# A decoder layer on one core: the first channels as two single chunks, three blocks held in PSUM, weights packed in 4 KB runs

## The chip, the cores and the metric

The kernel runs on one core of a Trainium2 chip. A core has five engines with queues of their own: TensorE (PE; PEld is its weight load), VectorE (DVE), ScalarE (ACT), GpSimd (POOL) and SyncE (SP), and 16 DMA engines that bring data from HBM into SBUF. TensorE writes its sums into PSUM, eight banks of 128 partitions x 512 floats. The metric is the device time of one execution in microseconds (us); a profiled execution gives the trace. In the profile, L156 is line 156 of the kernel before, "whi" and "wlo" are the two halves of a weight, "acc" and "misc" are PSUM banks.

## What is computed

One layer of a hybrid decoder, 256 tokens by 2048 channels, all in float32:

```python
mod = silu(c) @ w_ada + b_ada                      # (1, 12288)
shift1, scale1, gate1, shift2, scale2, gate2 = split(mod, 6)
h = rms_norm(x, norm1_gain) * (1 + scale1) + shift1
proj = h @ w_in                                    # 2048 -> 13840 columns
# stick-breaking attention, dilated attention and gated linear attention on columns of proj,
# each projected to 2048, gated by sigmoid(gate columns of proj), summed
x = x + gate1 * (mixed @ w_out)
h = rms_norm(x, norm2_gain) * (1 + scale2) + shift2
gate, up = split(h @ w_ffn_in, 2)
x = x + gate2 * ((silu(gate) * up) @ w_ffn_out)
```

## The kernel before

**Matmuls.** Each float32 factor is split in two: `hi`, rounded to TensorE's fast float32 format, and `lo`, the rest. A product is three matmuls, hi x hi, hi x lo and lo x hi (`mm3`, lines 153 to 156). A *block* is 512 output columns; its two token tiles of 128 accumulate in two PSUM banks. A *chunk* is 128 input channels. One chunk of one block is thus six matmuls of 128 x 512. `load_weights` (lines 125 to 151) loads two chunks (512 KB) with one DMA on SP's queue into one of four `raw` buffers; ScalarE casts them to `whi` (L148), DVE subtracts to get `wlo` (L149). There are four buffers of each.

**The input projection.** The normalised input needs shift1 and scale1, for which 16 tiles of w_ada for every channel chunk must be read and multiplied by silu(c). So that the projection can start early, its 16 channel chunks go in groups, `GROUPS` = (0,3), (3,7), (7,11), (11,16). One pass over 13 blocks uses one group; meanwhile `ada_group` (lines 277 to 310) reads w_ada for the next one (L291) and DVE multiplies and adds (L269, L271), spread over the pass; then TensorE turns the sums (L321), DVE reduces them (L322) and finishes shift and scale (L328, L331), and `make_h` (lines 424 to 436) writes hi (L429) and lo (L436) of h, both tiles of a chunk at once. A block's result of the first pass is copied by ScalarE from PSUM to SBUF (`A[b]`, L473); the next passes add theirs to it on DVE (L475). In the last pass ScalarE copies `A[b]` into the PSUM banks before the block (L461, "seeded"), and the matmuls add to that. The last block of a pass stays in PSUM and is the first of the next ("carried").

**The start.** `first_group` (lines 487 to 553) issues on SP's queue: three tiles of w_ada for chunks 0 to 2 (384 KB each), the first weight tile, x (four DMAs of 512 KB, L375), the other 13 tiles of w_ada. `norm1` (lines 380 to 411) sums the squares of x on ScalarE (L387), makes 1/rms, puts it on a scaled identity (L404), and TensorE multiplies x by it, which transposes and scales x (L410); ScalarE copies the result to `xT` (L411). DVE adds the 16 products, columns of chunk 0 last by themselves; ones sum them over the partitions (L313), and h of chunk 0 follows; chunks 1 and 2 go by way of transposes (L538) and sums (L541). Between these, `keep_warm` (lines 413 to 417) lets TensorE multiply ones, 78 matmuls in all, whose result nobody reads.

**PSUM.** Four banks are "acc" (the blocks), four "misc" (everything else).

**The order of the work.** Each engine runs its own instructions in a fixed order, which a scheduler made from priorities (`prio`) and the edges that `issue_after` adds. The weights, x and w_ada all go through SP's queue in this order; the small vectors through SP's and GpSimd's.

**Later.** The last pass has the two attentions and the gated linear attention between its blocks; the r blocks (columns 13 and 14, `gla`'s output gate) and the 12 gate blocks follow with all 16 chunks at once; then the branch projections, `w_out`, and the feed-forward part.

Of the kernel before, what the change touches and what calls it, by code (L numbers as in the profile page):

```python
# [17 lines left out]
P = 128  # L18
# [15 lines left out]
DEFER = 4  # L34
AHEAD = 4000
WARM = (22, 43, 10, 3)
FIN = 13
GROUPS = ((0, 3), (3, 7), (7, 11), (11, 16))
# [3 lines left out]
ROW_N1, ROW_N2, ROW_SBQ, ROW_SBK, ROW_DILQ, ROW_DILK, ROW_GB, ROW_GG = 16, 32, 48, 49, 50, 51, 52, 56  # L42
# [24 lines left out]
def trunk(ctx: ExitStack, tc: tile.TileContext, I, out):  # L67
# [57 lines left out]
    def load_weights(src, k0, k1, c0, w=NB, spare=(), ahead=True):  # L125
# [32 lines left out]
    def block(pss, act, src, k0, k1, c0, base=0, w=None, tiles=range(NT), go_on=False, more=False, seeded=False):  # L158

        if w is None:  # L160
            w = load_weights(src, k0, k1, c0)
# [27 lines left out]
    nc.scalar.preload_act_table_set("natural_log_exp_and_others")  # L189
# [7 lines left out]
    nc.sync.dma_start(crow[0:KC, :], by_chunk("c"))  # L197
# [12 lines left out]
    vec = const.tile([P, 58], F32, name="vec")  # L210
    bada = const.tile([P, 96], F32, name="bada")

    def load_vectors():
        nc.sync.dma_start(rows[16:32, :], by_chunk("norm1_gain"))
        nc.sync.dma_start(brow[0:96, :], by_chunk("b_ada"))
        nc.sync.dma_start(rows[32:48, :], by_chunk("norm2_gain"))
        with tc.issue_after(made):
# [9 lines left out]
            nc.gpsimd.dma_start(rows[0:16, :], by_chunk("c"))  # L227

    def turn_vectors():
        cols_ps = misc_bank([P, 64])  # L230
        nc.tensor.transpose(cols_ps[:, :58], rows[:58, :], ident[:58, :58])
        nc.scalar.copy(vec, cols_ps[:, :58])
        bada_ps = misc_bank([P, 96])
        state["row_turn"] = nc.tensor.transpose(bada_ps, brow[:96, :], ident[:96, :96])
        nc.scalar.copy(bada, bada_ps)
# [28 lines left out]
    w_ada = I["w_ada"]  # L264
# [12 lines left out]
    def ada_group(k0, k1, tags=ADA_TAGS, between=None):  # L277
# [5 lines left out]
        for i in range(pieces):  # L283
# [4 lines left out]
            for k in range(KC):  # L288
                with prio():
                    raw = S(tags[count % len(tags)], [P, 2, w])  # L290
                    nc.sync.dma_start(  # L291
                        raw,
                        w_ada[k * P : (k + 1) * P, : 2 * D].rearrange("p (s c) -> p s c", s=2)[:, :, a * P : a * P + w],
                    )
# [53 lines left out]
    def ada_segment_steps(acc, seg, done):  # L348


        for k in range(KC):
            for j in range(2):
# [3 lines left out]
                c0 = seg * D + j * 2 * NB  # L356
# [23 lines left out]
    def norm1():  # L380
# [21 lines left out]
        for t in range(NT):  # L402
            act(col(r, t), col(y, t), AF.Copy, scale=col(z, t))
            act(diag[:, t, :], ident, AF.Copy, scale=col(r, t))  # L404
        for j in range(4):
            for t in range(NT):
                ps = misc_bank([P, 4, P])
                for i in range(4):
                    xs = xin[2 * t + j // 2][:, j % 2, i * P : (i + 1) * P]
                    state["turn"] = nc.tensor.matmul(ps[:, i, :], xs, diag[:, t, :], start=True, stop=True)  # L410
                state["turned"] = nc.scalar.copy(xT[j][:, :, t * P : (t + 1) * P], ps)  # L411

    def keep_warm(n):

        ps = acc_bank()
        for _ in range(n):
            state["warm"] = nc.tensor.matmul(ps, ones_r, wide, start=True, stop=True)
# [26 lines left out]
    A = [None] * 13  # L444

    up, down = list(range(13)), list(range(12, -1, -1))
    orders = (up[1:] + up[:1], up, down)
# [4 lines left out]
    def proj_block(g, b, w=None, carry=False):  # L452
        k0, k1 = GROUPS[g]
        go_on = bool(carried)
        pss = carried.pop() if go_on else [acc_bank() for _ in range(NT)]
        seeded = g == LAST and not go_on
        if seeded:

            with prio():
                for t in range(NT):  # L460
                    nc.scalar.copy(pss[t], A[b][:, t, :])  # L461
            go_on = True
        block(pss, h_at, w_in, k0, k1, b * NB, w=w, go_on=go_on, more=carry, seeded=seeded)
        if carry:
            carried.append(pss)
            return
        with prio():
# [3 lines left out]
            for t in range(NT):  # L471
                if first or seeded:
                    nc.scalar.copy(A[b][:, t, :], pss[t])  # L473
                else:
                    nc.vector.tensor_add(A[b][:, t, :], A[b][:, t, :], pss[t])  # L475

# [10 lines left out]
    def first_group():  # L487


        k0, n = GROUPS[0]  # L490
        w = n * P
        tags = tuple(f"A{j}" for j in range(9)) + ADA_TAGS
        raws = []

        def load(ks):
            for k in ks:
                raw = S(tags[k % len(tags)], [P, 2, w])
                nc.sync.dma_start(raw, w_ada[k * P : (k + 1) * P, : 2 * D].rearrange("p (s c) -> p s c", s=2)[:, :, :w])
                raws.append(raw)

        load(range(0, 3))
        early.extend(load_weights(w_in, 0, 2, orders[0][0] * NB, ahead=False))
        split = state["split"]
        load_x()
        load(range(3, KC))
        with tc.issue_after(c_turn.ins):
            keep_warm(WARM[0])
        with tc.issue_after(state["warm"].ins):
            turn_vectors()
        with tc.issue_after(state["row_turn"].ins):  # L510
            keep_warm(WARM[1])
        norm1()
        with tc.issue_after(state["turn"].ins):
            keep_warm(WARM[2])
        acc = S("ada", [P, 2, w])
        for k in range(KC - 1):
            with tc.issue_after(split.ins) if k > 3 else nullcontext():
                ada_mac(acc, raws[k], k)
        sh, sc = mod1[:, 0, 0:n], mod1[:, 1, 0:n]
        chunk = lambda q: slice(q * P, (q + 1) * P)  # L520

        def last_mac(q):
            return ada_mac(acc[:, :, chunk(q)], raws[KC - 1][:, :, chunk(q)], KC - 1)

        last_mac(0)
        last_mac(1)
        behind = state["warm"]
        for q in range(n):
            if q == 0:
                sums = misc_bank([P, 2])  # L530
                for j in range(2):
                    with tc.issue_after(behind.ins):
                        behind = column_sum(sums[:, j : j + 1], acc[:, j, chunk(q)])
            else:
                ps = misc_bank([P, 2, P])
                for j in range(2):
                    with tc.issue_after(behind.ins):
                        behind = nc.tensor.transpose(ps[:, j, :], acc[:, j, chunk(q)], ident)  # L538
                sums = small([P, 2])
                with tc.issue_after(state["h_lo"].ins):  # L540
                    nc.vector.reduce_sum(sums, ps, axis=AX.X)  # L541
            finish_columns(sums[:, 0:1], sh[:, q : q + 1], SEG_SHIFT1, q)
# [748 lines left out]
```

## Time and profile before

| | |
|---|---|
| median of 3 runs | 1621.04 us (1619.27 to 1621.42) |
| the profiled execution, from first to last instruction | 1619.6 us |
| TensorE clock granted, mean | 0.998 |
| HBM read | 392.53 MB |
| moved by the DMA engines | 395.94 MB, mean 244 GB/s |
| DMA issues of w_in | 205 of 512 KB, 26 of 256 KB |

The page's busy shares are means over stages with different limits. A matmul's recorded length includes its way through the array, and matmuls overlap: the spacing of their starts, not the length, says how fast they go.

### The profile page before, as it was taken

To read this page: it belongs to the slowest core of one execution; us is meant where nothing else is said; L and a number is where in the kernel's file an instruction comes from. 1 tells how busy PE (TensorE), PEld (TensorE's weight loads), DVE (VectorE), ACT (ScalarE), POOL (GpSimd) and SP (SyncE) were. 2 spreads that over 40 slices of the span, in tenths; PEclk is the share of its full clock that TensorE was granted. 3 is DMA by queue.
4 is the path that set the end of the run, shared out by engine and by line. 5 is a ranking of instruction groups with operands and counts; after the bars stand their busy time and mean duration, and the time that the engine had idled before them with its cause. 6 is when DMAs were issued, how large, how long until landed. Compare 5 with 4: busy or idle time off the path is not lost.

```text
span 1619.6 us, 19955 instructions
## 1 busy us (share of the span) xinstructions
PE 1602.4 (99%) x7353; PEld 1324.3 (82%) x7353; DVE 1123.5 (69%) x1301; ACT 798.8 (49%) x1110; POOL 5.3 (0%) x14
## 2 busy tenths in 40 slices
PE   8999999999999999999999999999999999999998
PEld 7878888788888888888887888888888888888887
DVE  6899995887888787878657566677655555454454
ACT  4654449755795434444445444444444444333332
POOL 1000000000000000000000000000000000000000
PEclk9999999999999999999999999999999999999999
DMA  9999997884876889898756577888666666666663
GB/s 321 339 336 321 330 313 241 283 263 131 272 235 221 302 304 311 304 305 302 237 191 202 152 240 254 276 269 263 207 190 187 189 188 187 190 206 193 206 207 111
DMA packets 194593, 395.94 MB, mean 244 GB/s; under 512 B 12914, under 2 KB 27928, under 8 KB 194496
## 3 DMA queue, kind: packets, MB, share of 16 engines
q1 hardware_dynamic: 194272, 394.67, 74.8%
q8 instruction: 57, 0.93, 0.2%
q14 instruction: 40, 0.33, 0.1%
q0 software_dynamic: 224, 0.01, 0.0%
HBM read 392.53 MB, written 2.10 MB: 244 GB/s over the span
## 4 chain that ended last, share of the span: by engine, by line
PE 87%; DVE 5%; DMA 3%; ACT 3%; issue 2%; SPq 0%; DVEq 0%; ACTq 0%
PE acc L156 27%; PE acc L154 27%; PE acc L155 27%; DVE wlo L149 2%; ACT whi L148 1%; DVE ada L271 1%; DMA AR<-w_ada 1%; PE misc L1061 1%; ACT scr L616 1%; PE misc L775 1%; DMA OS<-w_ada 1%; DMA A<-w_ada 1%; DVE T L271 0%; DMA raw<-w_br_gla 0%; DMA raw<-w_in 0%
## 5 line engine op out<-in xcount | busy, mean ns | idle before, releaser
L149 DVE TENSOR_TENSOR wlo<-raw,whi 128x1024 fp32r<-128x1024 f32 (+1 forms) x546 | 651.6, 1198 | 421.4 <-ACT whi L148 420.2
L148 ACT CAST whi<-raw 128x1024 fp32r<-128x1024 f32 (+1 forms) x546 | 562.5, 1032 | 703.5 <-PE acc L156 583.1
L154 PE MATMUL acc<-whi,H 128*128 128x512 f32 x1576 | 616.6, 392 | 0.4 <-ACT H L1143 0.4
L156 PE MATMUL acc<-whi,H 128*128 128x512 f32 x1576 | 616.0, 391 | 1.0 <-DVE H L1144 0.6
L155 PE MATMUL acc<-wlo,H 128*128 128x512 f32 x1576 | 615.7, 391 | 1.0 <-DVE wlo L149 1.0
L156 PEld LDWEIGHTS acc<-whi,H 128*128 128x128 f32 x1576 | 296.1, 188 | 63.1 <-DVE H L436 1.5
L155 PEld LDWEIGHTS acc<-wlo,H 128*128 128x128 f32 x1576 | 296.4, 188 | 61.8 <-DVE wlo L149 1.8
L154 PEld LDWEIGHTS acc<-whi,H 128*128 128x128 f32 x1576 | 296.4, 188 | 60.3 <-ACT H L1143 0.6
L154 PE MATMUL acc<-whi,A 128*128 128x512 f32 x312 | 121.9, 391 | 0.0
L155 PE MATMUL acc<-wlo,A 128*128 128x512 f32 x312 | 121.5, 389 | 0.3 <-DVE wlo L149 0.3
L156 PE MATMUL acc<-whi,A 128*128 128x512 f32 x280 | 109.0, 389 | 0.0
L271 DVE SCALAR_TENSOR_TENSOR ada<-AR,csil,ada 128x1024 f32<-128x1024 f32 x59 | 75.1, 1278 | 5.8 <-DMA AR<-w_ada 5.8
L155 PEld LDWEIGHTS acc<-wlo,A 128*128 128x128 f32 x312 | 58.6, 188 | 12.7 <-DVE wlo L149 0.7
L154 PEld LDWEIGHTS acc<-whi,A 128*128 128x128 f32 x312 | 58.6, 188 | 11.9
L156 PEld LDWEIGHTS acc<-whi,A 128*128 128x128 f32 x280 | 52.6, 188 | 11.0
L154 PE MATMUL acc<-whi,T 128*128 128x512 f32 x120 | 46.7, 389 | 0.0
L155 PE MATMUL acc<-wlo,T 128*128 128x512 f32 x120 | 46.7, 389 | 0.0
L156 PE MATMUL acc<-whi,T 128*128 128x512 f32 x120 | 46.7, 389 | 0.0
L156 PE MATMUL acc<-whi,OS 128*128 128x512 f32 x112 | 43.6, 389 | 0.0
L271 DVE SCALAR_TENSOR_TENSOR ada<-OS,csil,ada 128x1024 f32<-128x1024 f32 (+2 forms) x33 | 35.5, 1077 | 1.8 <-DMA OS<-w_ada 1.5
L473 ACT COPY A<-acc 128x512 f32<-128x512 f32 x50 | 29.0, 586 | 10.2 <-PE acc L156 9.1
L475 DVE TENSOR_TENSOR A<-A,acc 128x512 f32<-128x512 f32 x48 | 31.5, 682 | 2.0 <-PE acc L156 1.8
(347 smaller groups left out, 1228.8 us busy)
## 6 DMA issues: line engine op xcount, KB each, us to landing
raw<-w_in SPq DMA_DIRECT2D x205, 512.0 KB, 5.3
raw<-w_ffn_in SPq DMA_DIRECT2D x176, 512.0 KB, 4.0
raw<-w_ffn_out SPq DMA_DIRECT2D x88, 512.0 KB, 4.7
AR<-w_ada SPq DMA_DIRECT2D x79, 512.0 KB, 5.3
raw<-w_out SPq DMA_DIRECT2D x32, 512.0 KB, 4.7
KC<-w_ada SPq DMA_DIRECT2D x30, 512.0 KB, 4.9
OS<-w_ada SPq DMA_DIRECT2D x16, 512.0 KB, 5.8
raw<-w_br_gla SPq DMA_DIRECT2D x16, 512.0 KB, 6.8
```

The source lines that it names most:

```text
L148: state["cast"] = nc.scalar.copy(hi[:, :n, :], raw[:, :n, :])
L149: state["split"] = nc.vector.tensor_tensor(lo[:, :n, :], raw[:, :n, :], hi[:, :n, :].bitcast(F32), op=ALU.subtract)
L154: nc.tensor.matmul(ps, lh, rh, start=start, stop=False, skip_group_check=seeded)
L155: nc.tensor.matmul(ps, lh, rl, start=False, stop=False, skip_group_check=seeded)
L156: state["mm"] = nc.tensor.matmul(ps, ll, rh, start=False, stop=stop, skip_group_check=seeded)
L271: nc.vector.scalar_tensor_tensor(acc, raw, c, acc, op0=ALU.mult, op1=ALU.add)
L473: nc.scalar.copy(A[b][:, t, :], pss[t])
L475: nc.vector.tensor_add(A[b][:, t, :], A[b][:, t, :], pss[t])
L616: nc.scalar.activation(junk, heads(b)[:, t, h, :], AF.Square, accum_out=ss[:, t, i : i + 1])
L775: nc.tensor.matmul(ps[:n, t * N_GLA + h, :].rearrange("p (s l) -> p s l", l=L), at(f, h, t)[:, :n], odd(at(f, h, t)), start=True, stop=True,)
L1061: nc.tensor.transpose(ps[:, i, :], src[:, i * P : (i + 1) * P], ident)
```

## The change

The pass groups become (0,2), (2,6), (6,10), (10,16). The last group's w_ada comes in two pieces of three chunks (`PIECES`).

- *Order of loads.* c, norm1_gain, b_ada and norm2_gain go to ScalarE's queue, ahead of its table load. SP's first loads are x, then w_ada of chunk 0 alone (four DMAs of 512 KB), half tiles of weights for two blocks and one full tile for a third, w_ada of chunk 1 (four DMAs), a last half tile for each of the first two.
- *Chunk 0 and chunk 1 apart.* Each has its own 16 products; of chunk 0, four are done on TensorE (`PE_KS`), and DVE does twelve. Sums over partitions are matmuls with ones for both.
- *Three blocks in PSUM.* When h of chunk 0 is there, blocks 1, 2 and 3 get its matmuls (18) into four acc banks and two misc banks, and stay. The remaining transposes of x, then chunk 1's sums follow in TensorE's order (`on_pe` chains them); then chunk 1 finishes the three blocks.
- *Warm-ups.* 24 instead of 78.
- *r blocks in pass 0.* Pass 0 has 15 blocks (13 and 14 too); the r blocks later are seeded and use chunks 2 to 15.
- *Seeds.* In pass 1 even blocks are seeded, in passes 2 and 3 all.
- *Layout.* The weights are laid out before the launch so that a tile of two chunks is one piece of HBM with 4 KB for each partition (2 KB before); w_ada of the first two segments likewise; the 16 columns `a_gla` of w_in as one array of 1 KB for each partition.

```diff
-WARM = (22, 43, 10, 3)
-FIN = 13
-GROUPS = ((0, 3), (3, 7), (7, 11), (11, 16))
+PE_KS = ((4, 5, 6, 7), ())
+WARM = (18, 6)
+FIN = (15, 13, 13, 13)
+GROUPS = ((0, 2), (2, 6), (6, 10), (10, 16))
+PIECES = ((2, 4), (6, 4), (10, 3), (13, 3))
...
-                nc.sync.dma_start(
-                    raw[:, :n, :],
-                    src[ka * P : (ka + n) * P, c0 : c0 + w].rearrange("(k p) c -> p k c", p=P),
-                )
+                nc.sync.dma_start(raw[:, :n, :], src[b, ka // 2])
...
-    nc.sync.dma_start(crow[0:KC, :], by_chunk("c"))
+    nc.scalar.dma_start(crow[0:KC, :], by_chunk("c"))
+    nc.scalar.preload_act_table_set("natural_log_exp_and_others")
...
+    def turn_x(diag, j, t):
+        ps = misc_bank([P, 4, P])
+        for i in range(4):
+            xs = xin[2 * t + j // 2][:, j % 2, i * P : (i + 1) * P]
+            on_pe(nc.tensor.matmul, ps[:, i, :], xs, diag[:, t, :], start=True, stop=True)
+        nc.scalar.copy(xT[j][:, :, t * P : (t + 1) * P], ps)
+
+    def on_pe(op, *args, **kw):
+        with tc.issue_after(state["pe"]):
+            state["pe"] = op(*args, **kw).ins
...
     def proj_block(g, b, carry=False):
         k0, k1 = GROUPS[g]
         go_on = bool(carried)
+        if go_on:
+            pss, seeded = carried.pop()
+        else:
+            pss = [acc_bank() for _ in range(NT)]
+            seeded = g > 0 and (g > 1 or b % 2 == 0)
+            if seeded:
+                seed(b, pss)
+                go_on = True
+        block(pss, h_at, w_in, k0, k1, b, go_on=go_on, more=carry, seeded=seeded)
...
     def first_group():
+        load_x()
+        raws = [[S(f"A{4 * q + j}", [P, 4, 2, P]) for j in range(4)] for q in range(2)]
...
+        for j in range(4):
+            load(0, j)
+        raw0 = tile_of(0)
+        raw1 = tile_of(2)
+        for j in range(4):
+            load(1, j)
+        raw2 = tile_of(1)
+
+        state["pe"] = c_turn.ins
+        keep_warm(WARM[0])
+        turn_vectors()
+        keep_warm(WARM[1])
...
+        sums = [misc_bank([P, 2]) for _ in range(2)]
...
+        products(0)
+        diag = norm1()
+        behind = macs_of(0, [k for k in range(KC) if k not in PE_KS[0]])
+        for t in range(NT):
+            turn_x(diag, 0, t)
+        finish_sums(0)
+        turn_x(diag, 1, 0)
+        w0, _ = halves_of(raw0, (slice(0, 1), slice(1, 2)), (state["diag"].ins, state["h_hi"].ins))
+        with tc.issue_after(state["h_hi"].ins), tc.issue_after(state["h_lo"].ins):
+            w1, split1 = halves_of(raw1)
+        pss = [[acc_bank() for _ in range(NT)], [acc_bank() for _ in range(NT)], [misc_bank([P, NB]) for _ in range(NT)]]
+        with tc.issue_after(state["pe"]):
+            for n, w in enumerate((w0[0], w0[1], w1[0])):
+                block(pss[n], h_at, None, 0, 1, 0, w=[w], more=True)
+        state["pe"] = state["mm"].ins
+        turn_x(diag, 1, 1)
+        for j in (2, 3):
+            for t in range(NT):
+                turn_x(diag, j, t)
+        macs_of(1, list(range(KC)), split1.ins)
+        finish_sums(1)
+        w2, _ = halves_of(raw2)
+        with tc.issue_after(state["pe"]):
+            for n, w in enumerate((w2[0], w2[1], w1[1])):
+                block(pss[n], h_at, None, 1, 2, 0, w=[w], go_on=True)
+                evacuate(blocks[n], pss[n], False)
...
-        for k in range(0, KC, 8):
-            raw = wp.tile([P, 8, P], F32, tag="raw", name=nm("raw"))
-            with prio():
-                nc.sync.dma_start(raw, w_in[k * P : (k + 8) * P, COL_A : COL_A + P].rearrange("(k p) c -> p k c", p=P))
+        raw = scr([P, KC, RANK])
+        with prio():
+            nc.sync.dma_start(raw, I["in_a"])
...
-        block(pss, h_at, w_in, 0, KC, (13 + j) * NB)
+        seed(13 + j, pss)
+        block(pss, h_at, w_in, 2, KC, 13 + j, go_on=True, seeded=True)
```

`evacuate` and `seed` are the copies that stood in `proj_block`; `finish_sums`, `products` and `macs_of` do what their names say for one chunk. `tile_of(0)` and `tile_of(1)` load the first and the second chunk of two blocks, `tile_of(2)` both chunks of the third.

More of the change, by code (lines that the diff above doesn't have):

```diff
@@ L443, in trunk, with evacuate @@
     w_in = I["w_in"]
-    A = [None] * 13
+    A = [None] * 15
     up, down = list(range(13)), list(range(12, -1, -1))
-    orders = (up[1:] + up[:1], up, down)
+    orders = (up[1:] + [13, 14] + up[:1], up, down)
     carried = []
     LAST = len(GROUPS) - 1
[L452 to L457, printed above, removed]
-            with prio():
[L460 to L466, printed above, removed]
+    def evacuate(b, pss, seeded):
         with prio():
@@ L487, in first_group @@
     def first_group():
[L490 to L495, printed above, removed]
-            for k in ks:
[L497 to L542, printed above, removed]
-            finish_columns(sums[:, 1:2], sc[:, q : q + 1], SEG_SCALE1, q, ROW_N1)
-            if q == 0:
-                with tc.issue_after(state["finish"].ins):
-                    last_mac(2)
-            make_h(q, sh[:, q : q + 1], sc[:, q : q + 1], True)
-            if q == 0:
-                with tc.issue_after(state["h_first"].ins):
-                    early.extend(load_weights(w_in, 2, n, orders[0][0] * NB, ahead=False))
@@ new lines, in products @@
+        def products(q):
+            for j in range(2):
+                for n, k in enumerate(PE_KS[q]):
+                    on_pe(
+                        nc.tensor.matmul, sums[q][:, j : j + 1], k_of(q, k)[:, j, :], csil[:, k : k + 1], start=n == 0 and j == 0,
+                        stop=False, skip_group_check=True,
+                    )
+        products(0)
[3 more added lines that the diff above has]
+            turn_x(diag, 0, t)
```

168 lines of the change are left out of this document (115 added, 53 removed).

## The prediction, made before the result was known

> **What bounds the kernel now.** I read the page first for the engine that carries the span.
>
> ```profile
> span 1619.6 us, 19955 instructions
> PE 1602.4 (99%) x7353; PEld 1324.3 (82%) x7353; DVE 1123.5 (69%) x1301; ACT 798.8 (49%) x1110; POOL 5.3 (0%) x14
> ```
>
> TensorE is busy 99%, but a busy TensorE need not be doing useful work, so I then cut the span into stages with the view of windows (columns: stage, length, busy us and instructions of PE, PEld, DVE, ACT, POOL, granted clock, DMA share, GB/s).
>
> ```profile
> 2.70:34.37 31.67, 29.21 (x154) 24.25 (x154) 19.66 (x31) 15.21 (x35) 2.29 (x5) 0.99 1.02 358
> 34.37:93.15 58.78, 57.79 (x252) 47.06 (x250) 49.20 (x62) 38.17 (x58) 0.00 (x0) 0.97 0.96 331
> 93.15:164.00 70.85, 70.47 (x315) 58.10 (x314) 67.74 (x78) 34.47 (x41) 0.00 (x0) 1.00 0.96 329
> 164.00:235.00 71.00, 71.00 (x320) 58.54 (x319) 69.83 (x92) 29.96 (x32) 0.00 (x0) 1.00 0.95 324
> 235.00:1619.60 1384.60, 1373.78 (x6320) 1136.22 (x6318) 916.31 (x1037) 679.70 (x945) 1.04 (x1) 1.00 0.72 230
> ```
>
> The first row is the start-up. The timeline says what TensorE does in it:
>
> ```profile
> 2.74 7.17 PE L417 MATMUL acc<-H,ones_r 128*128 128x512 f32 x22
> 10.53 10.27 PE L417 MATMUL acc<-H,ones_r 128*128 128x512 f32 x43
> 20.64 4.62 PE L410 MATMUL misc<-H,A 128*128 128x128 f32 x40
> 27.70 2.58 PE L417 MATMUL acc<-H,ones_r 128*128 128x512 f32 x10
> 34.37 0.63 PE L154 MATMUL acc<-whi,H 128*128 128x512 f32 x1
> 34.79 0.63 PE L155 MATMUL acc<-wlo,H 128*128 128x512 f32 x1
> ```
>
> L417 multiplies ones to keep the clock up; only L410, the transposes of x, is needed. The first projection matmul starts at 34.37. From 235 us on, 10.8 of 1384.6 us are idle, and the change leaves that work as it is. So two things can move: when the projection's work starts, and whether it then flows until it is the same as before. What is spent inside a warm block of matmuls is fixed:
>
> ```profile
> 78.03 0.39 PE L156 MATMUL acc<-whi,H 128*128 128x512 f32 x1
> 83.92 0.39 PE L155 MATMUL acc<-wlo,H 128*128 128x512 f32 x1
> 93.15 0.39 PE L154 MATMUL acc<-whi,H 128*128 128x512 f32 x1
> 94.15 0.74 PE L156 MATMUL acc<-whi,H 128*128 128x512 f32 x2 [0.39 <-DVE H L436]
> ```
>
> The first two rows are 26 starts apart: 5.89 / 26 = 0.2265 us for each matmul (the 0.39 is a latency). At 93.15 the second channel group enters; I use that point as S and compare S before and after. Before it stand 13 blocks x 3 chunks x 6 = 234 matmuls; after the change 15 blocks x 2 chunks x 6 = 180. The other 54 matmuls run later, which costs 54 x 0.2265 = **12.2 us**. The gain is 93.15 - S(after) - 12.2.
>
> **The first chunk.** The start-up now needs x, chunk 0 of w_ada, and one small weight tile, not x and all three chunks. Rows of its chain:
>
> ```profile
> 2.58 1.46 SPq L498 DMA_DIRECT2D A<-w_ada  x3
> 4.60 2.15 SPq L375 DMA_DIRECT2D A<-x  x4
> 15.75 1.06 ACT L387 ACTIVATE H<-A 128x1024 f32<-128x1024 f32 x1
> 19.53 0.70 ACT L404 ACTIVATE H<-ident,tiny 128x128 f32<-128x128 f32 x2
> 30.97 0.88 DVE L271 SCALAR_TENSOR_TENSOR ada<-A,csil,ada 128x256 f32<-128x256 f32 x2
> 32.29 0.22 DVE L328 TENSOR_TENSOR mod<-misc,bada 128x1 f32<-128x1 f32 x2 [0.43 <-PE misc L313]
> 32.54 0.16 DVE L331 SCALAR_TENSOR_TENSOR mod<-mod,vec 128x1 f32<-128x1 f32 x1
> 32.80 0.60 ACT L429 ACTIVATE H<-T,mod 128x256 fp32r<-128x256 f32 x1 [4.23 <-DVE mod L331]
> 4.00:10.00 6.00, 5.91 (x20) 4.32 (x19) 1.64 (x2) 0.00 (x0) 0.99 (x2) 1.00 0.98 322
> 10.00:15.00 5.00, 4.73 (x21) 3.89 (x22) 2.15 (x2) 4.26 (x7) 0.00 (x0) 1.00 1.01 392
> 15.00:30.00 15.00, 15.00 (x99) 13.34 (x97) 11.51 (x14) 9.65 (x26) 0.00 (x0) 1.00 1.06 378
> 40.00:84.00 44.00, 44.00 (x195) 36.07 (x194) 36.99 (x36) 28.25 (x43) 0.00 (x0) 1.00 0.98 341
> ```
>
> The bulk of the transfers begins about 1.5 us after the first large issue (2.58, against the window from 4 us on). c and the vectors leave SP's queue for ScalarE's, so x is issued at some 0.8 and flows from 2.3. Sizes: x is 256 x 2048 x 4 B = 2.10 MB; one chunk of shift and scale is 2048 x 256 x 4 B = 2.10 MB. At 360 GB/s, my value between the rows' 322 and 392, x is there at about 8.7, chunk 0 at 14.5. From the start of the last square (15.75) to the scaled identity (19.53 + 0.70) are 4.5 us; so that is ready at 13.3. DVE adds twelve of the sixteen products of chunk 0 (four go to TensorE as matmuls with one column). The last four after landing: 4 x 0.4 = 1.6 (row: 0.88 for two), to 16.1. From there to the first h are 32.80 + 0.60 - 31.40 = 2.0 us in the rows; I take 2.0 again, and 0.4 for two groups of x's transposes that now stand ahead of these sums. First projection matmul at about **18.5**, not 34.4. The removed warm-ups (78 to 24) were never on this chain.
>
> The 18 matmuls of chunk 0 (three blocks, six accumulators) start cold: 34.37 to 34.79 is 0.42 us each. With nine of them cold and nine at 0.2265 they take 5.8 us, to 24.3. [...]
>
> **The second chunk.** Two limits. DVE: split of two weight tiles, then 16 products of chunk 1, held back behind the second split (about 20.4): 16 x 0.4 = 6.4, to 27. TensorE: behind the 18 matmuls stand five more groups of transposes of x, in TensorE's fixed order, and only behind them the sums of chunk 1. Of the four misc banks two hold the third block and one the second sums, so one is left: each group costs four matmuls, its ScalarE copy and the hand-overs.
>
> ```profile
> L410 PE MATMUL misc<-H,A 128*128 128x128 f32 x64 | 7.3, 275 | 0.0
> L411 ACT COPY T<-misc 128x512 f32<-128x512 f32 x8 | 4.7, 586 | 3.7 <-PE misc L410 3.7
> L149 DVE TENSOR_TENSOR wlo<-raw,whi 128x1024 fp32r<-128x1024 f32 x15 | 18.3, 1222 | 9.9 <-ACT whi L148 9.9
> L148 ACT CAST whi<-raw 128x1024 fp32r<-128x1024 f32 x15 | 15.7, 1048 | 16.4 <-DMA raw<-w_in 16.3
> L271 DVE SCALAR_TENSOR_TENSOR ada<-OS,csil,ada 128x1024 f32<-128x1024 f32 x8 | 10.2, 1280 | 0.1
> ```
>
> Eight groups took 7.3: 0.9 each, in a warm array. With one bank a group also waits for the copy of the one before (0.59) and two hand-overs (0.25, an estimate: from DVE to ScalarE it is 0.1, 32.70 to 32.80): 5 x 0.9 + 4 x 0.84 = 7.9. With several banks free it is 5 x 0.9 = 4.5; in a cold array, at twice 0.9, 12.4. I take 7.9: sums of chunk 1 at 32.2, and its h, by the 1.1 from 32.29 (the first add behind the sums) to 33.40 that the old pass needed, at about **33**.
>
> **The rest of pass 0.** Three limits from 33 on:
> - TensorE: 18 matmuls (4.1, or 5.9 cold), 12 blocks x 12 x 0.2265 = 32.6, eight transposes 1: done at 71 to 72.5.
> - DVE: 16 products of four chunks (16 x 1.28 = 20.5) and 12 splits (12 x 1.22 = 14.6): 35 us. Starts overlap their predecessors by some 0.08, 2 us in all; I take half of that off and leave half for waits on casts: 34, from the low half of h at 33.6 to 67.6.
> - Transfers: x, two chunks, three early tiles (1.57 MB), four chunks (8.39), ten of twelve blocks (10 x 0.524): 21.5 MB by the last product. 2.3 + 21.5 / 0.36 = 62; at 341, 65.
>
> So DVE sets the last product, and the transfers are there before. Behind its last product comes a chain, read from the old pass:
>
> ```profile
> 80.97 2.60 DVE L271 SCALAR_TENSOR_TENSOR ada<-OS,csil,ada 128x1024 f32<-128x1024 f32 x2
> 84.38 1.03 PE L321 MATMUL misc<-ident,ada 128*128 128x128 f32 x8
> 91.00 0.42 DVE L436 TENSOR_TENSOR H<-scr,H 128x256 fp32r<-128x256 f32 x1
> ```
>
> From the transposes to the first h of the next group are 91.42 - 84.38 = 7.0 us. Before, two whole blocks (36 matmuls, 8.2 us) covered it; now two blocks are 5.4 us, so the chain shows. S(after) = 67.6 + 0.4 + 7.0 = **75.0**. Gain: 93.15 - 75.0 - 12.2 = **6.0 us** (5.95).
>
> **Passes 1 and 2.** Pass 1 is 13 x 24 x 0.2265 = 70.7 us for 22.0 MB (311 GB/s): less than ran before. Pass 2 now prepares six chunks: 13.6 + 12.6 = 26.2 MB in the same time, 371 GB/s, between the 341 and the 378 to 392 of the rows. Six product buffers and four weight buffers (4.5 MB) carry over what pass 1 leaves; I take nothing. DVE's load falls: adds move to ScalarE's seeds, all in pass 2, half in pass 1 (682 ns x 26 = 18 us of its 69.83). The 4 KB runs cover transfers that end long before they are needed (DMA share 0.72 behind 235): nothing. r blocks with two chunks done early: the same matmuls. One packed load for the gate columns takes the place of two loads of 0.52 MB: nothing on TensorE.
>
> The sum is on the profiled execution, 1619.6; the runs' median is 1621.04, 1.4 above its span, and I carry the gain over: 1621.04 - 6.0 = **1615.0**.
>
> **Rivals.**
> - *Nothing shows in the start-up.* Turns overlap, so h of chunk 1 is there at 29 and DVE runs without gaps (33 us to 62.6); half of the chain hides behind blocks: S = 29 + 4.1 + 32.6 + 1 = 66.7 by TensorE, 62.6 + 0.4 + 4 = 67 by DVE, gain 14, **1607**. For it: 4 KB runs flow best (the 392 is the window of x). Against: the old DVE waited 9.9 us for casts.
> - *Transfers bind passes 0 and 2.* At 341 pass 2 takes 26.2 / 0.341 = 76.8, 6.1 more than its matmuls: 1615.0 + 6.1 = **1621**, no change. For it: the share of 0.98 at 341. Against: that rate was with 2 KB runs, and x did better. [...]
> - *Seeds become the bound.* A seeded block cannot start until ScalarE has emptied its bank and refilled it: two evacuations, two seeds (0.59 each), between them up to two casts (1.05): 4.5 us with no hand-overs, inside a block of 5.44. If casts or the h work push it past 5.44, every seeded block (6 of pass 1, 12 of pass 2) waits; 0.6 us each is 11 us: **1626**. It eats the gain at 0.33 a block and is slower beyond measurement from 0.5 on. Against: the old last pass seeded every block, with 6.8 us for each, and TensorE was idle 0.15 us:
>
> ```profile
> 236.00:300.00 64.00, 63.85 (x297) 52.26 (x296) 42.47 (x57) 55.89 (x130) 1.04 (x1) 1.00 0.81 257
> ```
>
> - *The change does little of what it says*: the turns run cold (12.4), chunk 1 comes at 37.5, later than the old first matmul, and the early chunk buys almost nothing: S is 79.5, gain 1.5, **1619.5**.
>
> **How the numbers follow.** Forecast 0.47, start-up in full 0.23, transfers 0.11, late chunk 0.11, seeds 0.08. What a measurement can tell from no change is about 0.2%, 3.2 us. Faster (under 1617.8): the first two and a little of the late chunk, 0.72; same: late chunk and transfers, 0.20; slower 0.08. Range: from the full start-up, 1607, less 0.5 for shorter hand-overs, to the transfers' 1621.
>
> **What would show it.** Right: first projection matmul near 18.5, a slow run of five groups of turns, chunk 1 near 33, DVE almost without gaps from there, S at 75, and passes 1 and 2 at 70.8 each. Wrong: gaps on TensorE ending on `acc` copies from A (seeds), on casts waiting for w_in beyond 90 us (transfers), or an h of chunk 1 after 36. A bigger gain would show as S below 70.

## The result, and the profile after

The changed kernel takes 1631.71 us, the median of 4 runs (1631.27 to 1632.74), against 1620.17 (1619.27 to 1621.42) before. The ratio is 1.0067 [1.0053, 1.0081]: slower by 0.67%, some 11.5 us. The forecast was 1615.0 with a range up to 1621; the sign is wrong. The ratios here and below leave out three executions that are far out of line: 2299.72 us of e3, at a granted clock of 0.751, and two of some 4179 us of the old kernel beside e5 to e7.

The page of the changed kernel, span and engines:

```profile
span 1630.9 us, 19818 instructions
PE 1603.4 (98%) x7317; PEld 1321.2 (81%) x7317; DVE 1105.4 (68%) x1257; ACT 832.2 (51%) x1173; POOL 4.8 (0%) x13
```

TensorE is busy as long as before (1603.4 against 1602.4), although 54 warm-up matmuls are gone; 10.3 of the 11.3 us of span are idle time, and the mean granted clock is lower (0.993 against 0.998). The view of windows, with the columns of the prediction, cuts the changed kernel at the points that the forecast spoke of: first chunk-1 matmul, transposes of the next group's sums, S.

```profile
34.98:78.49 43.51, 37.77 (x134) 28.47 (x135) 31.35 (x27) 24.54 (x36) 0.00 (x0) 0.87 0.82 278
78.49:88.74 10.25, 9.91 (x45) 7.48 (x44) 8.62 (x13) 7.53 (x13) 0.00 (x0) 1.00 0.62 200
88.74:164.00 75.26, 74.39 (x332) 61.03 (x331) 67.19 (x73) 47.74 (x66) 0.00 (x0) 1.00 0.92 331
164.00:235.00 71.00, 70.44 (x313) 57.06 (x313) 57.58 (x67) 54.43 (x84) 0.00 (x0) 1.00 0.89 313
```

The first row, from chunk 1 to the transposes, stands out. In it no engine is full: TensorE is idle 5.7 of 43.5 us, DVE busy 31.4, ScalarE 24.5, the DMA engines at 0.82, and the granted clock is 0.87. Something makes the engines wait for each other. The marks come from the timeline of TensorE in the changed kernel (start, length, instruction, and in brackets the idle time before it and what ended it):

```profile
20.46 0.50 PE L154 MATMUL acc<-whi,H 128*128 128x512 f32 x1
...
24.78 4.72 PE L416 MATMUL misc<-H,A 128*128 128x128 f32 x40
...
34.98 0.79 PE L154 MATMUL acc<-whi,H 128*128 128x512 f32 x1 [1.07 <-ACT H L434]
...
78.49 1.03 PE L319 MATMUL misc<-ident,ada 128*128 128x128 f32 x8
...
88.74 0.39 PE L154 MATMUL acc<-whi,H 128*128 128x512 f32 x1
...
90.22 0.74 PE L156 MATMUL acc<-whi,H 128*128 128x512 f32 x2 [0.86 <-DVE H L441]
```

S, the row that I took for the entry of the second group, lies in both kernels eight matmuls behind the group's true first matmul (1.8 us before; 2.4 in the changed kernel, where a wait of 0.29 falls between). The comparison holds, since it is the same place in each.

| us | forecast | changed kernel |
|---|---|---|
| first projection matmul | 18.5 | 20.46 |
| first chunk-1 matmul | 33 | 34.98 |
| from there to the transposes | 35.0 | 43.51 |
| transposes to S | 7.0 | 10.25 |
| S | 75.0 | 88.74 |
| S to the end, over before's 1526.45 | +12.2 | +15.7 (1630.9 - 88.74 = 1542.16) |

The errors that add up are 2.0 (up to chunk 1; the late first matmul is part of it), 8.5, 3.25 and 3.5 us, 17.3 in all: the 6.0 us of forecast gain turned into 11.3 of loss. Half of it lies in the stage from chunk 1 to the transposes. The view of waits on TensorE, in 34.98 to 78.49 (wait, total, times, longest):

```profile
PE acc L154 <- ACT whi L148: 4.2, 3, 1.6
PE acc L155 <- DVE wlo L149: 1.6, 3, 0.5
```

TensorE waits for weights that are not yet cast or split; these waits are its idle time in the stage. ScalarE's timeline shows why they are late:

```profile
60.59 1.99 ACT L148 CAST whi<-raw 128x1024 fp32r<-128x1024 f32 x2
65.99 0.59 ACT L465 COPY A<-acc 128x512 f32<-128x512 f32 x1 [3.40 <-PE acc L156]
67.12 0.59 ACT L465 COPY A<-acc 128x512 f32<-128x512 f32 x1 [0.55 <-PE acc L156]
69.17 1.27 ACT L465 COPY A<-acc 128x512 f32<-128x512 f32 x2 [1.45 <-PE acc L156]
70.33 1.99 ACT L148 CAST whi<-raw 128x1024 fp32r<-128x1024 f32 x2
```

and TensorE's beside it:

```profile
61.69 0.73 PE L154 MATMUL acc<-whi,H 128*128 128x512 f32 x2 [1.62 <-ACT whi L148]
62.95 0.50 PE L155 MATMUL acc<-wlo,H 128*128 128x512 f32 x1 [0.53 <-DVE wlo L149]
...
64.47 0.63 PE L154 MATMUL acc<-whi,H 128*128 128x512 f32 x1
64.90 0.63 PE L155 MATMUL acc<-wlo,H 128*128 128x512 f32 x1
...
71.43 0.73 PE L154 MATMUL acc<-whi,H 128*128 128x512 f32 x2 [1.62 <-ACT whi L148]
```

ScalarE casts two blocks' weights (60.59), then stands 3.40 us with nothing to do, because next in its queue are the copies out of PSUM of the two blocks that TensorE is just working on; the casts for the blocks after them come behind those copies (70.33). So TensorE finishes what it has, then waits for copy, cast and split: at 53.53, 61.69 and 71.43. One round of two blocks takes 70.33 - 60.59 = 9.74 us, where their 24 matmuls need 5.44. The clock falls too: some 2 us behind each of the two waits of 1.62 us begins a stretch of seven starts that are 0.43 us apart, like those at 64.47 and 64.90, not 0.2265. Before the change, and in the changed kernel, ScalarE's instructions stand in its queue like this (number, line, operation; the number behind a name is a buffer's, and the copies' acc tells the block):

```
before                              after
63 L148 CAST whi_739                58 L148 CAST whi_563
64 L148 CAST whi_745                59 L148 CAST whi_589
65 L473 COPY A_163<-acc_694         60 L465 COPY A_129<-acc_559
66 L473 COPY A_163<-acc_695         61 L465 COPY A_129<-acc_560
67 L148 CAST whi_777                62 L465 COPY A_136<-acc_585
68 L148 CAST whi_783                63 L465 COPY A_136<-acc_586
69 L473 COPY A_174<-acc_735         64 L148 CAST whi_618
70 L473 COPY A_174<-acc_736         65 L148 CAST whi_644
```

Before, the casts 739 and 745 of the block in acc_735 stand ahead of the copies of the block before it, acc_694: one block of lookahead. After, the cast 618 stands behind the copies of both blocks that are under way (the cast 563 feeds acc_559, 589 feeds acc_585): none. Up to block 7 the changed kernel still has the lookahead; it is lost from block 8 on, whose cast is the one that TensorE waits for at 53.53. Why the scheduler came to this order, no run shows.

### The profile page after: what moved, and what is told of

Its sections match the earlier page's. It is cut to its first block, busy times and chain, and to the rows that moved or that the text cites. A ratio compares the mean times of both kernels' runs of the same rounds, so it can differ in the third digit from the quotient of the medians.

```text
span 1630.9 us, 19818 instructions
## 1 busy us (share of the span) xinstructions
PE 1603.4 (98%) x7317; PEld 1321.2 (81%) x7317; DVE 1105.4 (68%) x1257; ACT 832.2 (51%) x1173; POOL 4.8 (0%) x13
## 4 chain that ended last, share of the span: by engine, by line
PE 92%; DVE 2%; DMA 2%; ACT 2%; issue 1%; SPq 0%; DVEq 0%; ACTq 0%
PE acc L155 29%; PE acc L156 29%; PE acc L154 29%; PE misc L1116 1%; DVE wlo L149 1%; ACT whi L148 1%; DMA AR<-ada_rest 1%; PE misc L830 1%; DMA raw<-w_in 0%; DMA A<-x 0%; DVE ada L551 0%; DVE ada L272 0%; PE misc L319 0%; DMA raw<-w_ffn_in 0%; PE misc L416 0%
## 5 line engine op out<-in xcount | busy, mean ns | idle before, releaser
L149 DVE TENSOR_TENSOR wlo<-raw,whi 128x1024 fp32r<-128x1024 f32 x530 | 647.9, 1225 | 452.4 <-ACT whi L148 450.6
L148 ACT CAST whi<-raw 128x1024 fp32r<-128x1024 f32 x530 | 556.6, 1053 | 630.5 <-PE acc L156 550.0
L465 ACT COPY A<-acc 128x512 f32<-128x512 f32 x88 | 51.2, 586 | 60.8 <-PE acc L156 59.3
L155 PEld LDWEIGHTS acc<-wlo,A 128*128 128x128 f32 x312 | 58.6, 188 | 12.1
L473 ACT COPY acc<-A 128x512 f32<-128x512 f32 x64 | 36.8, 592 | 0.6
L272 DVE SCALAR_TENSOR_TENSOR ada<-OS,csil,ada 128x1024 f32<-128x1024 f32 (+1 forms) x30 | 34.7, 1156 | 0.2
```

What stands on the lines that cost most here:

```text
L148: state["cast"] = nc.scalar.copy(hi[:, :n, :], raw[:, :n, :])
L149: state["split"] = nc.vector.tensor_tensor(lo[:, :n, :], raw[:, :n, :], hi[:, :n, :].bitcast(F32), op=ALU.subtract)
L155: nc.tensor.matmul(ps, lh, rl, start=False, stop=False, skip_group_check=seeded)
L272: nc.vector.scalar_tensor_tensor(acc, raw, c, acc, op0=ALU.mult, op1=ALU.add)
```

## The experiments

The theory (A) was this order; the rivals were the layout and the transfers (B), the seeds (C) and the cold start of chunk 1, whose matmuls start 0.43 us apart from 35.57 to 39.41 in the changed kernel. Each experiment is an edit of the changed kernel; "before" is the old kernel in runs on the same chip.

**e1, casts ahead of the copies.** In pass 0 a block's two copies are issued only behind the next block's cast.

```diff
         block(pss, h_at, w_in, k0, k1, b, go_on=go_on, more=carry, seeded=seeded)
+        let_go(0)
...
-        evacuate(b, pss, seeded)
+        if g > 0:
+            evacuate(b, pss, seeded)
+            return
+        held.append((b, pss))
...
+    def let_go(n):
+        while len(held) > n:
+            with tc.issue_after(state["cast"].ins):
+                evacuate(*held.pop(0), False)
```

> Theory A (ScalarE's fixed order: in pass 0 the casts of the next two blocks stand behind the PSUM copies of the two blocks that TensorE is still working on): with the copies of a block placed behind the cast of a later block, pass 0 runs without gaps from 35 us on, the second group enters at 75 to 79 us instead of 88.7, and the time falls by 10 to 13 us to 1619 to 1622. Theory B (transfers: weights stand in SP's queue behind w_ada tiles that wait for DVE): the casts still wait, now for their loads; the second group enters within 2 us of 88.7, the time is 1629 to 1632.

Measured: 1621.98 us, 1.0002 [0.9992, 1.0012] of before. e1's windows, cut at the same marks:

```profile
34.31:68.50 34.19, 33.32 (x135) 26.03 (x136) 31.07 (x27) 24.25 (x36) 0.00 (x0) 0.95 0.95 343
68.50:78.75 10.25, 9.91 (x46) 7.48 (x45) 8.62 (x13) 7.84 (x13) 0.00 (x0) 1.00 0.79 262
```

and ScalarE in its timeline:

```profile
56.95 1.27 ACT L465 COPY A<-acc 128x512 f32<-128x512 f32 x2 [0.50 <-PE acc L156]
58.11 1.05 ACT L148 CAST whi<-raw 128x1024 fp32r<-128x1024 f32 x1
```

The waits on TensorE in the stage, in e1:

```profile
PE acc L154 <- ACT H L434: 1.1, 1, 1.1
PE acc L155 <- DVE wlo L149: 0.9, 3, 0.4
```

The built programs of e1 and the changed kernel differ in the order of ScalarE's queue from the cast of block 8 on, and in nothing else: TensorE's, DVE's, GpSimd's and SP's orders are the same. Now a block's copies come behind the next block's cast, no wait for whi is left, the stage takes 34.19 us instead of 43.51 with the same work, and S moves from 88.74 to 78.75. Up to the cast of block 8 the two kernels go alike (17.0 us from the first chunk-1 matmul to 52.00, and to 51.30 in e1); the whole difference lies behind it, first in the changed kernel, then in e1:

```profile
52.00:78.49 26.49, 20.75 (x71) 14.89 (x70) 17.08 (x15) 13.91 (x20) 0.00 (x0) 0.87 0.79 261
51.30:68.50 17.20, 16.34 (x70) 12.49 (x69) 16.38 (x14) 12.36 (x19) 0.00 (x0) 1.00 0.99 369
```

In the whole stage TensorE's idle time fell from 5.7 to 0.9 us; the time that the clock took went from 43.51 x 0.13 = 5.7 to 34.19 x 0.05 = 1.7. Together these are 8.8 of the 9.3 us (roughly, as some of the idle time is itself at the low clock). The order of ScalarE's queue thus costs about 10 of the 11.5 us. B is answered by this run too: the weights come in the same order, and the casts no longer wait.

**e2, runs of 2 KB.** The weights are laid out, and read, in runs of 2 KB as before the change; all else, each engine's order too, stays.

```diff
-                nc.sync.dma_start(raw[:, :n, :], src[b, ka // 2])
+                nc.sync.dma_start(raw[:, :n, :], src[b, ka // 2].rearrange("k p c -> p k c"))
...
-    return np.stack([... .reshape(k, 2, P, NB).transpose(0, 2, 1, 3) ...])
+    return np.stack([... .reshape(k, 2, P, NB) ...])
```

> Only the run length of the weight tiles is undone (2 KB instead of 4 KB for each partition, the tiles still contiguous); every engine's order is the changed kernel's. Theory A: weights lie some 10 us in SBUF before their cast, so the time is that of the changed kernel within 1 us, 1631 to 1633. Theory B: transfers that take longer show at once in pass 0; 5 us or more slower.

Measured: 1631.74 us, 1.0058 [1.0043, 1.0073]. Its transposes come at 78.25 (78.49 in the changed kernel). The length of the weights' runs makes no difference here that these runs can tell, and with e1 B falls. (The layout of w_ada was not undone by itself.)

**e3, seeds in the last pass only.**

```diff
-            seeded = g > 0 and (g > 1 or b % 2 == 0)
+            seeded = g == LAST
```

> Seeds only in the last pass, as before; passes 1 and 2 add on DVE. Theory A: pass 0 stays as it is, 88 to 90 us; passes 1 and 2 hardly change, 1630 to 1634. Rival C (seeds hold TensorE up in passes 1 and 2): the 3.5 us by which the changed kernel is longer behind the second group's entry go, 1628.

Measured: 1633.85 us, 1.0065 [1.0049, 1.0082]: nothing gained. Its waits on TensorE from 90 to 240 us:

```profile
PE acc L155 <- DVE wlo L149: 2.4, 1, 2.4
```

Without the seeds DVE has the adds again, and a split comes 2.4 us late, at 219.12, in pass 2. In the changed kernel this line has 0.2. From S to the end it is 1632.1 - 89.6 = 1542.5 us, where the changed kernel has 1542.16, so the 3.5 us behind S are not the seeds'; C falls.

**e4, copies of pass 0 on DVE.**

```diff
             for t in range(NT):
-                if first or seeded:
+                if first:
+                    nc.vector.tensor_copy(A[b][:, t, :], pss[t])
+                elif seeded:
```

> The PSUM copies of pass 0 go to DVE; ScalarE's order then holds casts alone. Theory A: the lockstep moves, since now the splits of two blocks stand behind the copies of the two before; the second group enters at 84 to 92 us, 1626 to 1635. Rival E (ScalarE simply has too much to do in pass 0): the second group enters below 80, 1622 or less.

Measured, in one run: 1651.46 us, far off what was expected. The waits on TensorE from 34 to 240 us say where it went:

```profile
PE acc L155 <- DVE wlo L149: 13.9, 8, 2.3
PE misc L319 <- DVE ada L272: 5.5, 3, 2.9
```

The casts are free now, but the splits and the products stand behind copies on DVE that wait for TensorE (5.6 us from the first chunk-1 matmul, at 35.70, to the transposes, at 88.01), and DVE's own load has grown to 46.65 us of these 52.3, from 31.35. So load and lockstep are mixed in this one run, and neither expectation had its size; it shows only that taking the copies from ScalarE is not enough.

**e5, chunk 1 warm.** e1, with eight matmuls of ones behind the turns of x.

```diff
+        hold = misc_bank([P, NB])
+        for _ in range(8):
+            on_pe(nc.tensor.matmul, hold, ones_r, wide, start=True, stop=True)
         macs_of(1, list(range(KC)), split1.ins)
```

> e1 with eight matmuls on ones behind the turns, while TensorE waits for the sums of chunk 1. If the cold clock at the start of chunk 1 is on the path: its first nine matmuls at 0.23 instead of 0.42 us, the second group enters 1.5 to 2 us ahead of e1's 78.75, and the time is 1.5 to 2 us below e1. If DVE's products and splits set the end of pass 0: the matmuls are fast, but the second group enters within 0.5 us of 78.75 and the time is e1's.

Measured: 1622.13 us, 1.0009 [0.9999, 1.0020]. TensorE's timeline in e5:

```profile
36.07 0.50 PE L154 MATMUL acc<-whi,H 128*128 128x512 f32 x1 [1.07 <-ACT H L434]
36.41 0.40 PE L155 MATMUL acc<-wlo,H 128*128 128x512 f32 x1
36.64 0.40 PE L156 MATMUL acc<-whi,H 128*128 128x512 f32 x1
```

The starts are 0.23 us apart where the other kernels' chunk 1 starts at 0.43; yet S is 78.85, as in e1. Chunk 1 itself came 1.8 us later here, which took the warm start back, so this run shows only that the pair of them changes nothing. Most of that delay is there before the ones: the first projection matmul is at 21.57, in e1 at 20.21. Such shifts are between executions: e3, whose edit touches nothing before pass 1, has chunk 1 at 36.04, the changed kernel at 34.98.

**e6, chunk 1 earlier.** e1, with four of chunk 1's products on TensorE, its twelve on DVE undisturbed by the third tile's split, and the third block first.

```diff
-PE_KS = ((4, 5, 6, 7), ())
+PE_KS = ((4, 5, 6, 7), (0, 1, 2, 3))
...
-        macs_of(1, list(range(KC)), split1.ins)
+        products(1)
+        macs_of(1, [k for k in range(KC) if k not in PE_KS[1]], split1.ins)
         finish_sums(1)
-        w2, _ = halves_of(raw2)
+        w2, _ = halves_of(raw2, late=state["h_lo"].ins)
         with tc.issue_after(state["pe"]):
-            for n, w in enumerate((w2[0], w2[1], w1[1])):
+            for n, w in ((2, w1[1]), (0, w2[0]), (1, w2[1])):
```

> e1 with four of chunk 1's sixteen products on TensorE, the split of the third weight tile moved behind h of chunk 1, and the third block first. DVE loses 4 x 0.5 + 1.2 us ahead of chunk 1's sums: its first matmul at 31 to 32 us instead of 34.3, the second group enters at 76 to 77, the time is 2 to 3 us below e1: 1617 to 1619 where before is 1620. If pass 0 is bound by transfers from there on: chunk 1 comes earlier, the second group does not, and the time is e1's.

Measured: 1621.49 us, 0.9997 [0.9986, 1.0009]. Chunk 1 came at 34.64, not at 31 to 32: the four products on TensorE take it from 31.17 to 33.1, behind the turns, and the first projection matmul was 1.3 us later than e1's in this profile (21.50). S is at 79.6, not at 76 to 77. e6's windows:

```profile
45.00:55.00 10.00, 9.38 (x40) 7.11 (x39) 9.96 (x9) 6.38 (x9) 0.00 (x0) 1.00 0.97 357
55.00:65.00 10.00, 9.61 (x42) 7.30 (x40) 9.93 (x10) 7.52 (x12) 0.00 (x0) 1.00 1.02 398
```

DVE is full here (9.96 and 9.93 of 10), as the forecast had it for the whole stage, and TensorE lacks half a microsecond in ten.

**e7, e6 and five matmuls of ones** (e5's edit behind `products(1)`).

> e6 and five warm matmuls behind chunk 1's products. If both effects add: second group at 74.5 to 76, the time 3 to 5 us below before, 1615 to 1617. If DVE sets the end of pass 0: e6's time.

Measured: 1624.58 us, 1.0018 [1.0005, 1.0031]. Chunk 1 is at 35.77 and S at 81.5: the ones delay TensorE's part of the sums by 1.2 us (34.20, in e6 32.98), and the clock was not warm in this profile all the same: chunk 1's starts are 0.43 us apart from 36.37 to 41.91.

**e8, half of DVE's products.** e1 with this:

```diff
-                        ada_mac(acc, raw, k)
+                        if k0 != 2 or k % 2 == 0:
+                            ada_mac(acc, raw, k)
```

> The kernel of e1 with half of the vector engine's products of the second channel group left out (every odd chunk of the sums, so the output's second half group is incomplete); its weight loads, casts and splits all stay, in their order. Theory A': with the casts ahead, pass 0 with two chunks is held up by the vector engine (9.93 of 10 us busy in the windows of e6): without some 8 products of 1.28 us in the stretch from the first matmul of chunk 1 to the transposes of the sums, S comes 3 to 6 us earlier than e1's 78.75, to 73 to 76, where TensorE's own work binds. Rival: the transfers of the weights set pass 0 (share 0.97 of the DMA engines): S stays at 78 to 79, and the vector engine shows gaps. The time of the whole means little here, since what comes behind S is the same: 1616 to 1622.

Measured, in one run of this incomplete kernel: 1617.59 us; S at 77.8. e8's windows and transposes:

```profile
45.00:55.00 10.00, 10.00 (x45) 7.93 (x44) 6.97 (x7) 7.48 (x12) 0.00 (x0) 1.00 0.92 309
55.00:65.00 10.00, 10.00 (x49) 8.19 (x48) 6.84 (x7) 7.40 (x11) 0.00 (x0) 1.00 1.01 385
```

```profile
64.34 1.03 PE L320 MATMUL misc<-ident,ada 128*128 128x128 f32 x8
```

With DVE at 70% TensorE is never idle in these windows, where it lacked 0.4 and 0.5 us in e1: DVE did hold up e1's TensorE a little, and the transfers, at a share of 0.92 to 1.01, did not. But S comes 1.0 us earlier, not 3 to 6. From chunk 1 (34.66) to the transposes there are 122 matmuls, 122 x 0.2265 = 27.6 us, and some 2 us of cold start (0.43 us from start to start, 35.25 to 37.81): 29.6, measured 29.7. TensorE's own work lies right behind DVE's.

**e9, r blocks out of pass 0.** e1 with this:

```diff
-FIN = (15, 13, 13, 13)
+FIN = (13, 13, 13, 13)
...
-    orders = (up[1:] + [13, 14] + up[:1], up, down)
+    orders = (up[1:] + up[:1], up, down)
...
-        seed(13 + j, pss)
-        block(pss, h_at, w_in, 2, KC, 13 + j, go_on=True, seeded=True)
+        block(pss, h_at, w_in, 0, KC, 13 + j)
```

> The kernel of e1 with the r blocks taken out of pass 0 (two chunks of them, 24 matmuls of 0.2265 us, go to the later pass with all their chunks, unseeded): 5.4 us of TensorE's work leave the stretch before S and come behind it. If the vector engine's products and splits set pass 0 (theory A'), S comes only 2 to 4 us earlier than e1's 78.75 and the whole takes 1 to 3 us more than e1, 1623 to 1625. If TensorE's own work set it, S comes 5.4 us earlier, to 73.3, and the whole is the same as e1, 1621 to 1622.5. If a loading of weights sets it, S moves by less than 1 us and the whole takes 5 us more, 1627.

Measured: 1624.83 us, 1.0023 [1.0011, 1.0035]. S is at 77.07, 1.7 us earlier for 24 matmuls (5.4 us) less, a little under the 2 to 4 expected; chunk 1 was 1.85 us later in this profile (36.16), so from there to S it is 3.5 us shorter. Time and S lie near what DVE as the bound of pass 0 gives, and away from the 5.4 of TensorE and from the 1627 of the loads. By these runs the matmuls that the change put into pass 0 cost less there than later, though narrowly: the intervals of e9 and e1 just touch.

## Why the prediction was wrong, by its steps

**The step that failed** is "So DVE sets the last product, and the transfers are there before", in the rest of pass 0. It came from three sums of work, of TensorE, DVE and the transfers, and the longest was taken as the time. ScalarE isn't among the three: with 24.5 busy us of 43.5 it looks harmless, and its busy time indeed is. But the sums hold only where each engine can run ahead of the others, and ScalarE's fixed order didn't let it. e1 shows it: with the order of casts and copies changed, and nothing else, the stage takes 34.19 us, against 35.0 forecast. So the sum was near and its condition was not met. That the two agree so well is in part luck. In e1 ten splits stand ahead of the last product, not twelve; DVE is busy 31.07 us, not 34, and waits for casts (2.2 us) fill most of the rest. Nor is DVE alone the limit there: TensorE is busy 33.32 us of the same stage, and in e5, where DVE's work begins 1.8 us later and TensorE's clock is warm (1.00 from 28 to 45 us), the transposes come at 68.60, only 0.1 later than in e1. The trace of before could have raised the question: there the cover between a block's last matmul and the need for the next cast was a block of 18 matmuls, 4.1 us, and it becomes one of 12, 2.7 us, against a copy, a cast and a split of 0.59 + 1.05 + 1.22 = 2.86. I counted the shorter blocks in DVE's load alone. But blocks of 12 are not the cause by themselves: e1 has the same blocks and no such wait.

**The other terms** were mis-sized, by 1 to 3.5 us each.

- *First projection matmul*, 18.5 against 20.46 (20.2 to 21.6 in these profiles). The sum had DVE's products of chunk 0 end at 16.1, with four of 0.4 us left when the last of w_ada lands. DVE's timeline of the changed kernel, and TensorE's of e1:

```profile
14.04 0.48 DVE L551 SCALAR_TENSOR_TENSOR ada<-A,csil,ada 128x256 f32<-128x256 f32 x1 [0.64 <-DMA A<-ada]
...
15.76 2.57 DVE L551 SCALAR_TENSOR_TENSOR ada<-A,csil,ada 128x256 f32<-128x256 f32 x5
```

```profile
18.48 0.61 PE L416 MATMUL misc<-ones_r,ada 128*128 128x1 f32 x4 [1.08 <-DVE ada L563]
```

  The fifth product waits for its tile until 14.04; behind it no load is waited for, but each product takes 0.5 us, small copies of the vectors stand between, and the last ends at 18.3. In e1 TensorE waits for that, and its first projection matmul is at 20.21. The other path to it was late as well: I let the last square of x begin when x is there, at 8.7 (2.3 + 2.10 / 0.36 is 8.1; the wait for x ends at 8.96), but three squares were still to be done then, as ScalarE's timeline of the changed kernel shows:

```profile
11.06 1.05 ACT L385 ACTIVATE H<-A 128x1024 f32<-128x1024 f32 x1
...
14.86 0.69 ACT L402 ACTIVATE H<-ident,tiny 128x128 f32<-128x128 f32 x2
```

  From the last one's start to the scaled identity it is 14.86 + 0.69 - 11.06 = 4.5, as in the sum. The transposes of x that need it end just before the sums begin, at 18.66, in the changed kernel, but over 1 us ahead of DVE in e1, which gains only 0.25 us by that.
- *First chunk-1 matmul*, 33 against 34.98. The sum had nine cold matmuls among the 18 of chunk 0, 5.8 us in all; no run shows nine there. In the changed kernel the starts are some 0.23 us apart from the second on, with one of 0.31 among them, and the turns begin 4.32 us behind the first (20.46 to 24.78); the most is eight starts 0.42 to 0.45 us apart, in e2 and in e4. The five groups of turns took 4.72 us, not 7.9: there was no wait for a bank. DVE was the limit instead, with this in its timeline:

```profile
23.61 0.35 DVE L549 TENSOR_SCALAR ada<-A,csil 128x256 f32<-128x256 f32 x1
23.99 5.69 DVE L551 SCALAR_TENSOR_TENSOR ada<-A,csil,ada 128x256 f32<-128x256 f32 x11
29.60 1.22 DVE L526 TENSOR_TENSOR wlo<-raw,whi 128x1024 fp32r<-128x1024 f32 x1
30.74 2.04 DVE L551 SCALAR_TENSOR_TENSOR ada<-A,csil,ada 128x256 f32<-128x256 f32 x4
```

  They begin at 23.61 where I had 20.4, take 0.5 each where I had 0.4, and the split of the third tile stands among them. So the sums began at 32.92, 0.7 later than forecast; from there to the matmul it is 2.06 us, where I took 1.1 from the first add behind the sums and left out the sums themselves. The rival of the late chunk had the lateness, 2 us of its 4.5, for a reason that wasn't there (cold turns).
- *Transposes to S*, 7.0 against 10.25, in the changed kernel and in e1 alike. Of the 3.25, 1.8 are my own mixing of marks: 7.0 runs to the first h of the group, S of before lies 8.77 behind its transposes. And the chain did not show at the entry: the first hi half was there 5.05 us behind the transposes (83.54), and TensorE came to it at 7.86 (86.35), since the transposes and 28 matmuls of pass 0 (6.3 us) stood in between. I had seen two blocks of 12 there; and in the old kernel, where I had two blocks of 18, it was 21 matmuls. Only a later low half was awaited, 0.86, behind S.
- *Behind S*, +12.2 against +15.7 in the changed kernel. The first 12.2 are the moved matmuls. Of the other 3.5, e1 has 1.4 (1618.8 - 78.75 = 1540.05) and e8 none (1615.8 - 77.8 = 1538.0). The 2.1 between the changed kernel and e1 can be found, since TensorE's order is the same in both: the changed kernel is behind e1 by 9.99 us at S, still by 9.93 at 225 and by 9.90 at 450, by 10.5 from 500 on and by 12.1 from 900 on. So passes 1 and 2 have no part in it. The last 1.6 us are lost at the second norm, where the granted clock is 0.83 from 890 to 900, behind two waits of 1.17 and 1.43 us. e1 has the same two waits (1.00 and 1.37) and a clock of 1.00 from 878 to 888. The order there is the same, so this is a difference between executions, not the work of e1's edit. The 1.4 that e1 has too are not found; the seeds are not it (e3).

**The rivals.** "Transfers bind" had the time nearest to e1's, 1621, but not by its reason, a pass 2 that waits for its loads: in the changed kernel TensorE waits 1.3 us in all from 90 to 240 us, none of it for a cast, and the window 164 to 235 has a DMA share of 0.89. "Seeds become the bound" was the only one that ended slower, at 1626, and its sign was right by accident; what it described, a ScalarE instruction that holds up another, is the cause, in pass 0 and with copies and casts. I had looked for ScalarE's order only where the change added instructions to it.

**What a right forecast would have been.** Had the casts stood ahead, the change would have been worth nothing: 1621.98 against 1621.75 for e1, not 6 us less. The gain of 93.15 - 78.75 = 14.4 us at S is eaten by the 12.2 of moved matmuls and 1.4 behind them. In pass 0 DVE and TensorE now lie close together (half of DVE's products less is worth 1.0 us at S in e8), and the DMA engines are 0.9 to 1.0 busy beside them, so that no single one of them is likely to have much left to give. None of the complete versions beats the old kernel beyond the interval.

## What to carry to other kernels

Sums of work by engine bound a stage only from below; before taking the longest one, follow the fixed order of each engine, the idle ones too, and ask what stands behind an instruction that waits for the engine that you want to keep fed. Where blocks get shorter, compare the new length of a block with the time of its whole hand-over (copy, cast, split), and let the preparation of the next block stand ahead of the clearing of this one. A stage in which no engine is full (TensorE, with 37.77 of 43.51 us or 87%, was the busiest here) and each waits for the next can be the sign of such a lockstep. Moving a few casts was then worth more than taking work away: 10.0 us at S here, against 1.0 for half of DVE's products.

## What was not expected of the hardware

The transfers of this one core went faster than any row of the old kernel that the forecast showed. The view of the DMA in the changed kernel from 0 to 70 us, in 40 equal slices of 1.75 us:

```profile
GB/s 0 178 398 285 350 412 414 415 404 412 407 410 397 406 414 396 412 407 414 400 201 232 162 370 255 372 318 386 372 410 342 358 241 328 363 309 94 243 232 246
```

From 8.8 to 35 us it holds 396 to 415 GB/s, where 392 was the highest row of before in the forecast, and 341 the rate in its pass. Over the same window, 8.75 to 35.00, the mean is 408 GB/s, in the old kernel 380. So the 341 GB/s, at a DMA share of 0.98, by which the rival of the transfers timed pass 2 was not the most that this core's DMA engines could move. The slices behind 35 us are those of the lockstep. Chunk 1 waited for DVE and not for these loads, so the rate did not show in the time.
